# One-hot and gated columns of a routed expert layer, built on VectorE from 16-bit pairs

## The chip, the cores and the metric

The kernel runs on one core of a Trainium2 chip. The metric is device microseconds of one launch, as the median of repeated runs. One more run is taken with the hardware profiler, and all rows below come from it. The engines are named as the profile names them: PE (matmul) and PEld (its weight loads), DVE (VectorE), ACT (ScalarE), POOL (GpSimd) and SP (the queue that issues most loads).

## The reference

Two transformer-like blocks run over 256 tokens of width 1024. The change lies wholly in the last part, the routed feed-forward layer of the second block:

```python
def chunk(xc):
    q = (xc @ w_q).reshape(tc, PEER_HEADS, 2, PEER_DQ // 2)
    s = jnp.einsum('thpd,hpkd->thpk', q, sub_keys).astype(F32)
    s_top, i_top = lax.top_k(s, PEER_TOPK)
    ...
    best, pos = lax.top_k(cand.reshape(tc, PEER_HEADS, PEER_TOPK * PEER_TOPK), PEER_TOPK)
    expert = jnp.take_along_axis(...)
    gate = jax.nn.softmax(best, axis=-1)
    ue = jnp.take(expert_u, expert, axis=0)
    ve = jnp.take(expert_v, expert, axis=0)
    h = jax.nn.gelu(jnp.einsum('thkd,td->thk', ue, xc).astype(F32), approximate=False)
    return jnp.einsum('thk,thkd->td', (gate * h).astype(xc.dtype), ve)
```

Each token has 8 heads with 16 experts each, that is 128 slots. An expert's number is 128 i + j, with i and j from 0 to 127, and there are 16,384 experts.

## The kernel before

The kernel gathers nothing. It computes the gelu of all experts for all tokens, multiplies each by its gate (zero where the token has not chosen the expert), and multiplies the result with all of `peer_v`. H holds that table with i on the partitions and (j, token) behind it, in two halves of 64 values of j, H0 and H1.

The stages of `peer` are:

- **queries** and `up(0)`: the slots' i, j and gate are found on DVE (`top_experts`), while PE computes H0. At its end the slots stand on the partitions: `ir` and `jr` hold i and j of each slot by token, `gb` the gate in two 16-bit parts.
- **`up(1)`**: PE computes H1 with 24 matmuls of 256 columns for a weight unit pair (L312 to L315). Beside it `steps(0)` applies the gates to H0.
- **`down(0)`**: PE multiplies H0 with `peer_v` into four banks `acc` (L1390, 12 matmuls of 512 columns for a unit). Beside it `steps(1)` applies the gates to H1.
- **`down(1)`**: the same product for H1, with no gating left beside it, and then the last normalisation.

A step of gating serves 8 tokens. `spread` writes a one-hot column of i for each slot and token, A (128 by 8 by 128), and of j, B (128 by 8 by 64), both by comparing a row of the numbers 0 to 127 (`iota`, 32-bit, in the tile `keep`) with the slot's value; both comparisons are on DVE (L1429, L1431). POOL then makes B times the gate, once for each 16-bit part of the gate (G, L1435). `gated` multiplies A with the two G on PE, 16 small matmuls for 8 tokens (L1444), and DVE multiplies the result into H (L1446). There are 32 such steps for each half, and they come at 0.6 steps for each weight unit.

PE works in three 32-bit passes, so every operand is split into a high and a low part. For weights ACT makes the high part (`whi`, L205) and DVE the low one (`wlo`, L207), one of each for a unit of 128 by 1024, with three buffers of each. For H in `down`, ACT makes the high part (L1405) and POOL the low one (L1406), one of each for two units, in four places of the tiles `u3`. The first pair of H0 takes the two buffers of A for its parts, since `u3` still holds the input of `up(1)`.

In the queries stage the order of DVE and POOL is that of the code. In the experts stages (`up(1)`, `down`) a scheduler orders each engine's instructions; an engine then takes them strictly in that order.

Of the kernel before, what the change touches and what calls it, by code (L numbers as in the profile page):

```python
# [8 lines left out]
F32 = mybir.dt.float32  # L9
F32R = mybir.dt.float32r  # L10
BF16 = mybir.dt.bfloat16
F16 = mybir.dt.float16
U32 = mybir.dt.uint32
AF = mybir.ActivationFunctionType
OP = mybir.AluOpType
# [3 lines left out]
T = 256  # L19
# [5 lines left out]
UP = 2.0 ** 15  # L25
# [148 lines left out]
class Kern:  # L174
# [95 lines left out]
    def manual(self, scope, engines):  # L270

        names = dict(D=mybir.EngineType.DVE, A=mybir.EngineType.Activation, P=mybir.EngineType.Pool, T=mybir.EngineType.PE)
        if engines:
# [804 lines left out]
    def heads(self, m):  # L1078
# [33 lines left out]
        def level(lv):  # L1112
            A = act.tile([128, 4, C], F32, tag="Alv", name="Alv", bufs=5)
            nc.gpsimd.tensor_tensor(A, AT, b4(f"lvt{lv}"), op=OP.mult)
            return A

        nc.gpsimd.tensor_tensor(four(Wt), AT, b4("lvt0"), op=OP.mult)
        nc.gpsimd.tensor_tensor(four(Wt), b4("id64"), four(Wt), op=OP.subtract)
        A = level(1)
        nc.vector.transpose(out=W, in_=Wt)  # L1120
        yield HEADS[1]
        cut = lambda t, c, h: t[h, c * C:c * C + C]
        for lv in range(1, 6):
            p = self.two_banks(WARM_LEVEL)
            self.quads(lambda c, h, b, i: mm(p[h, b, i * C:i * C + C], A[h, c], cut(W, c, h), start=True, stop=True))
            X = act.tile([128, T], F32, tag="X", name="X", bufs=4)
# [69 lines left out]
    def chunks(self):  # L1196
# [6 lines left out]
        for c in range(4):  # L1203
# [15 lines left out]

            G = cut(self.sg, c)  # L1220
            if c:
                p = products((query(0), of(S0)))
                G = act.tile([128, 4, C], F32, tag="G", name="G", bufs=1)
                nc.vector.tensor_tensor(two(G), p, two(cut(self.sg, c)), op=OP.add)
                yield .5
# [130 lines left out]
    def peer(self, s):  # L1356
        tc, nc = self.tc, self.nc
# [3 lines left out]
        pp = e(tc.tile_pool(name="peer", bufs=1))  # L1361
# [5 lines left out]
        acc = [ps.tile([128, 512], F32, name=f"acc{i}") for i in range(4)]  # L1367


        ir, jr = (pp.tile([128, T], F16, name=n) for n in ("ir", "jr"))  # L1370
        gb = [pp.tile([128, T], F16, name=f"gb{n}") for n in range(2)]
        HJ = 64
        H = [None, None]
        H[0] = e(tc.tile_pool(name="h0", bufs=1)).tile([128, HJ, T], F32, name="H0")
        gp = e(tc.tile_pool(name="gp", bufs=1))
        mm = nc.tensor.matmul
# [15 lines left out]
        def down(half):  # L1392

            tail = []
            for i in range(HJ // 2):
                if half and i == HJ // 2 - 4:
                    nc.scalar.activation(ss[:, 0, 0:1], H[1][:, 2 * i, 0:1], AF.Square)
                    nc.scalar.activation(ss[:, 0, 0:1], ss[:, 0, 0:1], AF.Sqrt)
                if half == i == 0:
                    wh, wl = (gp.tile([128, 8, 128], F16, tag="A", name="A", bufs=2).rearrange("p a b -> p (a b)")  # L1400
                              .bitcast(F32R).rearrange("p (a t) -> p a t", a=2) for _ in range(2))
                else:
                    wh, wl = ((self.u3[n].rearrange("p (a b) t -> p a b t", b=2))[:, i % 4, :, :T] for n in range(2))
                src = H[half][:, 2 * i:2 * i + 2]
                nc.scalar.copy(wh, src)  # L1405
                nc.gpsimd.tensor_tensor(wl, src, wh.bitcast(F32), op=OP.subtract)  # L1406
                for u in range(2):
                    hi, lo = self.unit()
                    first = half + i + u == 0
                    todo = [(w[:, u], v) for w, v in ((wh, hi), (wl, hi), (wh, lo))]  # L1410
                    if half and i >= HJ // 2 - LAST:
                        tail.append(todo)
                        continue
                    for n, (w, v) in enumerate(todo):
                        for a in range(4):
                            products(a, w, v, first and n == 0, False)

            for a in range(4):
                for j, todo in enumerate(tail):
                    for n, (w, v) in enumerate(todo):  # L1420
                        products(a, w, v, False, j == len(tail) - 1 and n == 2)

        def spread(half, g):

            io, t8 = self.c("iota"), slice(g * 8, g * 8 + 8)
            A = gp.tile([128, 8, 128], F16, tag="A", name="A", bufs=2)
            B = gp.tile([128, 8, HJ], F16, tag="B", name="B", bufs=1)
            bc = lambda t, n: t[:, t8, None].to_broadcast([128, 8, n])
            nc.vector.tensor_tensor(B, io[:, None, half * HJ:half * HJ + HJ].to_broadcast([128, 8, HJ]),  # L1429
                                    bc(jr, HJ), op=OP.is_equal)  # L1430
            nc.vector.tensor_tensor(A, io[:, None, :].to_broadcast([128, 8, 128]), bc(ir, 128), op=OP.is_equal)  # L1431
            parts = []
            for n in range(2):
                G = gp.tile([128, 8, HJ], F16, tag=f"G{n}", name="G", bufs=2)
                nc.gpsimd.tensor_tensor(G, B, bc(gb[n], HJ), op=OP.mult)  # L1435
                parts.append(G)
            return A, parts

        def gated(half, g, A, parts):

            p = grp().rearrange("p (t j) -> p t j", t=8)
            for t in range(8):
                for n in range(2):
                    mm(p[:, t], A[:, t], parts[n][:, t], start=n == 0, stop=n == 1)  # L1444
            h = H[half][:, :, g * 8:g * 8 + 8]
            nc.vector.tensor_tensor(h, p.rearrange("p t j -> p j t"), h, op=OP.mult)  # L1446

# [46 lines left out]
        self.rest()  # L1494
        self.bg = steps(1)
        down(0)
        self.rest()
        self.save("H0", H[0])
# [42 lines left out]
    def top_experts(self, tk, sc, grp, ir, jr, gb, tt):  # L1541

        nc = self.nc
        v = nc.vector
# [21 lines left out]
        def pairs(h):  # L1566
            scr = tk.tile([128, 256], F32, tag="scr2", name="scr2", bufs=2)
            top16(bv[:, h], bi[:, h], cand[0][:, h], scr)
# [20 lines left out]
        def softmax():  # L1589
            g = tk.tile([128, 8, 16], F32, tag="gate", name="gate", bufs=1)  # L1590
            z = tk.tile([128, 8], F32, tag="z", name="z", bufs=1)
            v.tensor_tensor(g, bv, bv[:, :, 0:1].to_broadcast([128, 8, 16]), op=OP.subtract)
            nc.scalar.activation(g, g, AF.Exp)
            v.tensor_reduce(z, g, axis=AX.X, op=OP.add)
            v.reciprocal(z, z)
            v.tensor_tensor(g, g, z[:, :, None].to_broadcast([128, 8, 16]), op=OP.mult)

            def by_slot():
                p = grp()
                ts = slice(tt * 128, tt * 128 + 128)  # L1600
                nc.tensor.transpose(p[:, 0:128], g, self.c("ident"))
                nc.scalar.activation(gb[0][:, ts], p[:, 0:128], AF.Copy, scale=UP)
                v.scalar_tensor_tensor(gb[1][:, ts], p[:, 0:128], UP, gb[0][:, ts], op0=OP.mult, op1=OP.subtract)
            self.at(2, by_slot)
        yield COST[2], softmax

        def index(p2, dst):
            n = tk.tile([128, 8, 16], U32, tag="n", name="n", bufs=1)
            nf = tk.tile([128, 8, 16], F32, tag="nf", name="nf", bufs=2)
            out = tk.tile([128, 8, 16], F32, tag="nfo", name="nfo", bufs=2)  # L1610
            if p2 == 0:
                v.tensor_scalar(n, bi, 4, None, op0=OP.logical_shift_right)
            else:
                v.tensor_scalar(n, bi, 15, None, op0=OP.bitwise_and)
            v.tensor_copy(nf, n)

            def part(g):
                hs = slice(2 * g, 2 * g + 2)
                q = tk.tile([128, 2, 16, 16], F32, tag="pick", name="q", bufs=2)
                v.tensor_tensor(q.rearrange("p h k a -> p (h k) a"),  # L1620
                                nf[:, hs].rearrange("p h k -> p (h k)")[:, :, None].to_broadcast([128, 32, 16]),
                                io16[:, None, :].to_broadcast([128, 32, 16]), op=OP.is_equal)
                nc.gpsimd.tensor_tensor(q, q, tf[:, hs, p2][:, :, None, :].to_broadcast([128, 2, 16, 16]), op=OP.mult)
                return lambda: v.tensor_reduce(out[:, hs], q, axis=AX.X, op=OP.add)

            rest = []
            for g in range(5):
                yield
                if rest:
                    rest.pop()()  # L1630
                if g < 4:
                    rest.append(part(g))

            def by_slot():
                p = grp()
                nc.tensor.transpose(p[:, 0:128], out, self.c("ident"))
                nc.scalar.copy(dst[:, tt * 128:(tt + 1) * 128], p[:, 0:128])
            self.at(2, by_slot)

        for p2, dst in ((0, ir), (1, jr)):  # L1640
# [61 lines left out]
```

## Time and profile before

| what | value |
|---|---|
| median of 3 runs | 1479.79 us (1479.5 to 1481.15) |
| profiled execution, its own time | 1475.88 us |
| its span in the profile | 1474.1 us |
| PE busy | 1407.1 us (95%) |
| DVE busy | 1154.1 us (78%) |
| ACT busy | 721.2 us (49%) |
| POOL busy | 613.2 us (42%) |
| granted TensorE clock, mean | 0.980 |

The span runs from the first to the last instruction; 1.8 us of the run lie around it. The profiled execution is 3.9 us shorter than the median of the others, so a change worked out on its rows is to be taken off the median as a difference. Busy time of PE is modelled for pipelined matmuls: one that stands alone shows its whole latency as busy.

### The profile page before, as it was taken

The numbers are of one execution on the slowest core, as the hardware profiler recorded it, in microseconds if no ns is written. First come the engines' busy times: TensorE is split into PE (matmuls) and PEld (weight loads), VectorE is DVE, ScalarE is ACT, GpSimd is POOL, SyncE is SP. The second block draws the span as 40 slices with busy tenths as digits, with TensorE's granted clock in tenths as the row PEclk, the third lists the DMA queues.
The fourth block names the chain that finished last, engine by engine and source line by source line (L and its number), as shares of the span: only waits on it lengthen the run. The fifth ranks groups of instructions, "written<-read, shape, count | busy, mean of one in ns | idle before, by whom it ended". The sixth has DMA issues, their size and how long they took to land. (4 is left out here: it accounts for less than half of the span.)

```text
span 1474.1 us, 27562 instructions
## 1 busy us (share of the span) xinstructions
PE 1407.1 (95%) x11208; PEld 1284.0 (87%) x11208; DVE 1154.1 (78%) x1775; ACT 721.2 (49%) x1078; POOL 613.2 (42%) x434
## 2 busy tenths in 40 slices
PE   9999999999879999899999999999998898999997
PEld 7889999999768888899998999999976666788886
DVE  6789999974798766689879779999599999744445
ACT  6575566563763333645544543443543433445443
POOL 2601042210664200223465646777288887323230
PEclk9999999999989998999999999999999999999999
DMA  8478858744322101544544455444644455655552
GB/s 320 152 252 282 311 196 284 238 163 147 126 86 66 52 30 53 205 147 169 200 144 172 172 172 172 161 160 168 214 159 157 157 171 173 221 183 196 177 196 86
DMA packets 40447, 253.83 MB, mean 172 GB/s; under 512 B 4736, under 2 KB 4992, under 8 KB 13440
## 3 DMA queue, kind: packets, MB, share of 16 engines
q1 hardware_dynamic: 38592, 246.79, 48.4%
q10 hardware_dynamic: 1728, 5.28, 1.0%
q8 instruction: 88, 1.44, 0.4%
q14 instruction: 39, 0.32, 0.1%
HBM read 249.96 MB, written 2.10 MB: 171 GB/s over the span
## 5 line engine op out<-in xcount | busy, mean ns | idle before, releaser
L205 ACT CAST whi<-raw 128x1024 fp32r<-128x1024 f32 (+1 forms) x418 | 435.7, 1046 | 527.2 <-PE psu L313 217.9
L207 DVE TENSOR_TENSOR wlo<-raw,whi 128x1024 fp32r<-128x1024 f32 (+1 forms) x389 | 526.2, 1363 | 166.4 <-ACT whi L205 164.1
L312 PE MATMUL psu<-u3hi,whi 128*128 128x256 f32 x1128 | 287.2, 287 | 4.6 <-DVE qe L520 4.6
L313 PE MATMUL psu<-u3lo,whi 128*128 128x256 f32 x1128 | 282.9, 284 | 0.0
L1435 POOL TENSOR_TENSOR G<-B,gb 128x512 f16<-128x512 f16 x128 | 237.0, 1870 | 95.2 <-DVE B L1429 53.8
L312 PEld LDWEIGHTS psu<-u3hi,whi 128*128 128x128 f32 x1128 | 215.8, 191 | 4.8 <-DVE qe L520 4.8
L313 PEld LDWEIGHTS psu<-u3lo,whi 128*128 128x128 f32 x1128 | 215.6, 191 | 0.0
L315 PE MATMUL psu<-u3hi,wlo 128*128 128x256 f32 x1128 | 182.0, 284 | 4.1 <-DVE wlo L207 3.7
L1406 POOL TENSOR_TENSOR u3lo<-H,u3hi 128x512 fp32r<-128x512 f32 x63 | 106.8, 1696 | 160.0 <-ACT u3hi L1405 160.0
L315 PEld LDWEIGHTS psu<-u3hi,wlo 128*128 128x128 f32 x1128 | 155.5, 191 | 5.1 <-DVE wlo L207 4.2
L1390 PE MATMUL acc<-wlo,u3hi 128*128 128x512 f32 x504 | 141.7, 401 | 14.4 <-DVE wlo L207 14.0
L207 POOL TENSOR_TENSOR wlo<-raw,whi 128x1024 fp32r<-128x1024 f32 x29 | 70.5, 2430 | 188.2 <-ACT whi L205 188.2
L1390 PE MATMUL acc<-whi,u3hi 128*128 128x512 f32 x504 | 142.5, 402 | 1.9 <-ACT whi L205 1.9
L1390 PE MATMUL acc<-whi,u3lo 128*128 128x512 f32 x504 | 139.0, 396 | 0.0
L1390 PEld LDWEIGHTS acc<-wlo,u3hi 128*128 128x128 f32 x504 | 94.3, 190 | 42.7 <-DVE wlo L207 21.7
L1390 PEld LDWEIGHTS acc<-whi,u3lo 128*128 128x128 f32 x504 | 95.3, 189 | 22.1
L1390 PEld LDWEIGHTS acc<-whi,u3hi 128*128 128x128 f32 x504 | 93.3, 191 | 21.5 <-ACT whi L205 2.0
L1431 DVE TENSOR_TENSOR A<-keep,ir 128x1024 f16<-128x1024 f32 x64 | 94.9, 1484 | 0.1
L312 PE MATMUL mm<-u3hi,whi 128*128 128x256 f32 (+1 forms) x312 | 82.3, 295 | 0.0
L1429 DVE TENSOR_TENSOR B<-keep,jr 128x512 f16<-128x512 f32 x64 | 64.0, 1000 | 22.2 <-POOL G L1435 22.2
L313 PE MATMUL mm<-u3lo,whi 128*128 128x256 f32 (+1 forms) x312 | 78.7, 284 | 0.0
L313 PE MATMUL mm<-flo,whi 128*128 128x256 f32 x272 | 67.6, 282 | 0.0
(431 smaller groups left out, 2660.4 us busy)
## 6 DMA issues: line engine op xcount, KB each, us to landing
raw<-in_w_fm SPq DMA_DIRECT2D x74, 1024.0 KB, 4.9
raw<-in_peer_u SPq DMA_DIRECT2D x64, 1024.0 KB, 4.8
raw<-in_peer_v SPq DMA_DIRECT2D x64, 1024.0 KB, 4.8
ada<-in_ada_w SPq DMA_DIRECT2D x40, 512.0 KB, 5.4
raw<-in_w_qkv SPq DMA_DIRECT2D x5, 1024.0 KB, 10.6
H<-in_ada_w SPq DMA_DIRECT2D x8, 512.0 KB, 3.9
raw<-in_w_qkv SPq DMA_DIRECT2D x4, 256.0 KB, 5.2
xd<-kr SPq DMA_DIRECT2D x1, 1024.0 KB, 10.0
```

Source lines behind the costliest of these rows:

```text
L205: self.nc.scalar.copy(hi, src)
L207: e.tensor_tensor(lo, src, hi.bitcast(F32), op=OP.subtract)
L312: mm(out, w[k][0], x[k][0], start=start and k == 0, stop=False)
L313: mm(out, w[k][0], x[k][1], start=False, stop=False)
L315: mm(out, w[k][1], x[k][0], start=False, stop=stop and k == n - 1)
L1390: mm(acc[a], w[:, tt * 128:tt * 128 + 128], v[:, dh * 512:dh * 512 + 512], start=start, stop=stop)
L1406: nc.gpsimd.tensor_tensor(wl, src, wh.bitcast(F32), op=OP.subtract)
L1429: nc.vector.tensor_tensor(B, io[:, None, half * HJ:half * HJ + HJ].to_broadcast([128, 8, HJ]), bc(jr, HJ), op=OP.is_equal)
L1431: nc.vector.tensor_tensor(A, io[:, None, :].to_broadcast([128, 8, 128]), bc(ir, 128), op=OP.is_equal)
L1435: nc.gpsimd.tensor_tensor(G, B, bc(gb[n], HJ), op=OP.mult)
```

## The change

Three things change in `peer`:

- **All operands of A, B and G become 16-bit.** A 16-bit copy of `iota` is made once on ACT (the tile `io`). The slots' values `ir`, `jr` and `gb` are kept twice, side by side, so that a slot's value is read as a pair of equal neighbours again and again, in place of one element again and again. The writers of these values (L1602, L1603 and L1637 of before) write each value twice. `jr` and `gb` lie in the tile `qe`, which the queries stage has read by then. A, B and G are contiguous by token as before, written in pairs.
- **Both products G go from POOL to DVE**, right behind B or a step later.
- **The low part of H in `down`** (L1406) **goes from POOL to DVE** too.

```diff
-        ir, jr = (pp.tile([128, T], F16, name=n) for n in ("ir", "jr"))
-        gb = [pp.tile([128, T], F16, name=f"gb{n}") for n in range(2)]
+        ir = pp.tile([128, T, 2], F16, name="ir")
+        room = self.qe.rearrange("p a t -> p (a t)").bitcast(F16).rearrange("p (a t b) -> p a t b", a=3, b=2)
+        gb, jr = room[:, 0:2], room[:, 2]
+        io = pp.tile([128, 128], F16, name="io")
+        nc.scalar.copy(io, self.c("iota"))
...
-                nc.gpsimd.tensor_tensor(wl, src, wh.bitcast(F32), op=OP.subtract)
+                nc.vector.tensor_tensor(wl, src, wh.bitcast(F32), op=OP.subtract)
...
-            bc = lambda t, n: t[:, t8, None].to_broadcast([128, 8, n])
-            nc.vector.tensor_tensor(B, io[:, None, half * HJ:half * HJ + HJ].to_broadcast([128, 8, HJ]),
-                                    bc(jr, HJ), op=OP.is_equal)
-            nc.vector.tensor_tensor(A, io[:, None, :].to_broadcast([128, 8, 128]), bc(ir, 128), op=OP.is_equal)
-            parts = []
-            for n in range(2):
-                G = gp.tile([128, 8, HJ], F16, tag=f"G{n}", name="G", bufs=2)
-                nc.gpsimd.tensor_tensor(G, B, bc(gb[n], HJ), op=OP.mult)
-                parts.append(G)
-            return A, parts
+            G = gp.tile([128, 2, 8, HJ // 2, 2], F16, tag="G", name="G", bufs=2)
+            pairs = lambda t: t.rearrange("p (a b) -> p a b", b=2)[:, None]
+            of = lambda t, n: t[:, t8, None].to_broadcast([128, 8, n // 2, 2])
+            nc.vector.tensor_tensor(B, pairs(io[:, half * HJ:half * HJ + HJ]).to_broadcast([128, 8, HJ // 2, 2]),
+                                    of(jr, HJ), op=OP.is_equal)
             for n in range(2):
+                nc.vector.tensor_tensor(G[:, n], B, of(gb[:, n], HJ), op=OP.mult)
+            nc.vector.tensor_tensor(A, pairs(io).to_broadcast([128, 8, 64, 2]), of(ir, 128), op=OP.is_equal)
...
-                nc.scalar.activation(gb[0][:, ts], p[:, 0:128], AF.Copy, scale=UP)
-                v.scalar_tensor_tensor(gb[1][:, ts], p[:, 0:128], UP, gb[0][:, ts], op0=OP.mult, op1=OP.subtract)
+                two = p[:, 0:128, None].to_broadcast([128, 128, 2])
+                nc.scalar.activation(gb[:, 0, ts], two, AF.Copy, scale=UP)
+                v.scalar_tensor_tensor(gb[:, 1, ts], two, UP, gb[:, 0, ts], op0=OP.mult, op1=OP.subtract)
...
-                nc.scalar.copy(dst[:, tt * 128:(tt + 1) * 128], p[:, 0:128])
+                nc.scalar.copy(dst[:, tt * 128:(tt + 1) * 128], p[:, 0:128, None].to_broadcast([128, 128, 2]))
```

PE's order is the same in both kernels, but for two of the first matmuls of `down(0)`. What moves stands on DVE and POOL.

First, DVE in the middle of `down(0)`, one step of gating with the units around it. The order of before (`keep` holds the 32-bit `iota`; H_10167 is H1):

```order
L1446 TENSOR_TENSOR H_10167<-psg,H_10167 128x64x8
L1431 TENSOR_TENSOR A<-keep,ir 128x1024
L1429 TENSOR_TENSOR B<-keep,jr 128x512
L207 TENSOR_TENSOR wlo<-raw,whi 128x1024 x2
L1446 TENSOR_TENSOR H_10167<-psg,H_10167 128x64x8
```

The order after the change (`qe` is where `jr` and `gb` lie now; H_10166 is H1, H_7313 is H0):

```order
L1449 TENSOR_TENSOR H_10166<-psg,H_10166 128x64x8
L1438 TENSOR_TENSOR G<-B,qe 128x512 x2
L1439 TENSOR_TENSOR A<-io,ir 128x1024
L1435 TENSOR_TENSOR B<-io,qe 128x512
L207 TENSOR_TENSOR wlo<-raw,whi 128x1024
L1410 TENSOR_TENSOR u3lo<-H_7313,u3hi 128x2x256
L207 TENSOR_TENSOR wlo<-raw,whi 128x1024
L1449 TENSOR_TENSOR H_10166<-psg,H_10166 128x64x8
```

The two products and the low part of H now stand in DVE's queue, between the product into H and the low parts of the weights.

Second, POOL in `down(0)` before (gb_7309 and gb_7310 are the two parts of the gate, H_7314 is H0):

```order
L1435 TENSOR_TENSOR G<-B,gb_7309 128x512
L1435 TENSOR_TENSOR G<-B,gb_7310 128x512
L1406 TENSOR_TENSOR u3lo<-H_7314,u3hi 128x2x256
L1435 TENSOR_TENSOR G<-B,gb_7309 128x512
L1435 TENSOR_TENSOR G<-B,gb_7310 128x512
```

POOL's last instructions after the change, which all belong to the queries stage:

```order
L1627 TENSOR_TENSOR q<-q,tf 128x512
L207 TENSOR_TENSOR wlo<-raw,whi 128x1024
L1627 TENSOR_TENSOR q<-q,tf 128x512 x3
L207 TENSOR_TENSOR wlo<-raw,whi 128x1024 x2
L1693 UNCONDITIONAL_BRANCH
```

POOL has nothing left to do in `up(1)`, `down(0)` and `down(1)`.

Third, DVE around the start of `down(0)`. Before:

```order
L1446 TENSOR_TENSOR H_7314<-psg,H_7314 128x64x8
L1429 TENSOR_TENSOR B<-keep,jr 128x512
L207 TENSOR_TENSOR wlo<-raw,whi 128x1024 x12
L1431 TENSOR_TENSOR A<-keep,ir 128x1024 x2
L1446 TENSOR_TENSOR H_10167<-psg,H_10167 128x64x8
```

After:

```order
L1449 TENSOR_TENSOR H_7313<-psg,H_7313 128x64x8
L1438 TENSOR_TENSOR G<-B,qe 128x512 x2
L1410 TENSOR_TENSOR A<-H_7313,A 128x512
L1435 TENSOR_TENSOR B<-io,qe 128x512
L207 TENSOR_TENSOR wlo<-raw,whi 128x1024 x10
L1410 TENSOR_TENSOR u3lo<-H_7313,u3hi 128x2x256 x2
L207 TENSOR_TENSOR wlo<-raw,whi 128x1024
L1410 TENSOR_TENSOR u3lo<-H_7313,u3hi 128x2x256 x2
L207 TENSOR_TENSOR wlo<-raw,whi 128x1024
L1439 TENSOR_TENSOR A<-io,ir 128x1024 x2
L1449 TENSOR_TENSOR H_10166<-psg,H_10166 128x64x8
```

The first low parts of H, which can be made only when `up(1)` has left `u3`, stand ahead of two low parts of weights now; on POOL nothing stood behind them but products of the gates.

## Rows read from the trace of the kernel before

**Rows 1.** Page, busy tenths in 40 slices of 36.9 us: PE, DVE, POOL.

```profile
PE   9999999999879999899999999999998898999997
...
DVE  6789999974798766689879779999599999744445
...
POOL 2601042210664200223465646777288887323230
```

**Rows 2.** Windows: start:end, length, busy us (count) of PE, PEld, DVE, ACT, POOL; clock.

```profile
861.00:1057.90 196.90, 196.90 (x2023) 195.41 (x2022) 172.28 (x157) 82.75 (x97) 120.21 (x66) 1.00 0.49 168
1057.90:1258.40 200.50, 178.66 (x1168) 135.77 (x1168) 186.97 (x152) 77.42 (x90) 164.81 (x90) 0.98 0.48 166
1258.40:1285.00 26.60, 26.60 (x109) 21.49 (x110) 20.98 (x22) 11.51 (x13) 6.14 (x5) 0.94 0.66 233
1285.00:1462.50 177.50, 177.50 (x772) 143.99 (x771) 77.22 (x64) 82.69 (x94) 48.98 (x29) 1.00 0.51 175
```

**Rows 3.** Waits, 1057 to 1260: waiter, releaser, total us, times, longest us.

```profile
PEld acc L1390 <- DVE wlo L207: 21.7, 18, 3.1
...
PE acc L1390 <- DVE wlo L207: 14.0, 13, 2.6
...
PEld L1444 <- DVE A L1431: 9.2, 12, 1.4
```

**Rows 4.** Chain of waits, 1057 to 1474: start us, us, what.

```profile
1065.55 0.64 PE psg L1444 x16
...
1071.37 0.48 PE psg L1444 x16
...
1258.37 76.72 PE acc L1390 x324
...
1335.97 126.49 PE acc L1390 x546
```

**Rows 5.** Groups by form, DVE, 1057.9 to 1258.4: busy us, mean ns, idle before.

```profile
L207 DVE TENSOR_TENSOR wlo<-raw,whi 128x1024 fp32r<-128x1024 f32 x53 | 83.0, 1584 | 2.6 <-ACT whi L205 2.6
L1431 DVE TENSOR_TENSOR A<-keep,ir 128x1024 f16<-128x1024 f32 x32 | 48.8, 1527 | 0.1
L1429 DVE TENSOR_TENSOR B<-keep,jr 128x512 f16<-128x512 f32 x29 | 37.9, 1307 | 10.3 <-POOL G L1435 10.3
L1446 DVE TENSOR_TENSOR H<-psg,H 128x512 f32<-128x512 f32 x30 | 20.3, 678 | 0.0
L496 DVE SCALAR_TENSOR_TENSOR H<-H 128x1024 f32<-128x1024 f32 x4 | 7.5, 1868 | 0.7 <-DMA H<-in_ada_w 0.7
```

**Rows 6.** Groups by form, POOL, the same stretch.

```profile
L1435 POOL TENSOR_TENSOR G<-B,gb 128x512 f16<-128x512 f16 x60 | 114.2, 1922 | 32.8 <-DVE B L1429 19.9 <-PE psg L1444 10.4 <-PE acc L1390 2.5
L1406 POOL TENSOR_TENSOR u3lo<-H,u3hi 128x512 fp32r<-128x512 f32 x30 | 52.0, 1736 | 26.7 <-ACT u3hi L1405 26.7
```

**Rows 7.** Timeline, DVE, 967 to 978: start us, us, instruction.

```profile
967.54 0.68 DVE L1446 TENSOR_TENSOR H<-psg,H 128x512 f32<-128x512 f32 x1
968.15 1.46 DVE L1431 TENSOR_TENSOR A<-keep,ir 128x1024 f16<-128x1024 f32 x1
969.52 0.68 DVE L1429 TENSOR_TENSOR B<-keep,jr 128x512 f16<-128x512 f32 x1
...
975.22 0.68 DVE L1429 TENSOR_TENSOR B<-keep,jr 128x512 f16<-128x512 f32 x1
975.82 1.21 DVE L207 TENSOR_TENSOR wlo<-raw,whi 128x1024 fp32r<-128x1024 f32 x1
976.96 0.68 DVE L1446 TENSOR_TENSOR H<-psg,H 128x512 f32<-128x512 f32 x1
```

**Rows 8.** Line L1429, 1057 to 1260: count, duration min/median/max ns.

```profile
L1429 DVE TENSOR_TENSOR B<-keep,jr x29: 676/1656/1684, 1070.5 to 1248.8; 128x512 f16<-128x512 f32 x29
```

**Rows 9.** Line L1435, the same stretch and columns.

```profile
L1435 POOL TENSOR_TENSOR G<-B,gb x60: 1039/2014/2023, 1066.2 to 1252.4; 128x512 f16<-128x512 f16 x60
```

**Rows 10.** Line L207, 130 to 160: an instruction of a quarter of wlo's size.

```profile
L207 DVE TENSOR_TENSOR mlo<-t,mhi x8: 410/412/418, 135.0 to 154.1; 128x256 fp32r<-128x256 f32 x8
```

More of the change, by code (lines that the diff above doesn't have):

```diff
@@ L1399, in down @@
                 if half == i == 0:
-                    wh, wl = (gp.tile([128, 8, 128], F16, tag="A", name="A", bufs=2).rearrange("p a b -> p (a b)")
+                    wh, wl = (gp.tile([128, 8, 64, 2], F16, tag="A", name="A", bufs=2).rearrange("p a b c -> p (a b c)")
                               .bitcast(F32R).rearrange("p (a t) -> p a t", a=2) for _ in range(2))
@@ L1423, in spread, with gated @@
         def spread(half, g):
-            io, t8 = self.c("iota"), slice(g * 8, g * 8 + 8)
-            A = gp.tile([128, 8, 128], F16, tag="A", name="A", bufs=2)
-            B = gp.tile([128, 8, HJ], F16, tag="B", name="B", bufs=1)
-            bc = lambda t, n: t[:, t8, None].to_broadcast([128, 8, n])
-            nc.vector.tensor_tensor(B, io[:, None, half * HJ:half * HJ + HJ].to_broadcast([128, 8, HJ]),
-                                    bc(jr, HJ), op=OP.is_equal)
-            nc.vector.tensor_tensor(A, io[:, None, :].to_broadcast([128, 8, 128]), bc(ir, 128), op=OP.is_equal)
-            parts = []
-            for n in range(2):
-                G = gp.tile([128, 8, HJ], F16, tag=f"G{n}", name="G", bufs=2)
-                nc.gpsimd.tensor_tensor(G, B, bc(gb[n], HJ), op=OP.mult)
-                parts.append(G)
-            return A, parts
-        def gated(half, g, A, parts):
+            t8 = slice(g * 8, g * 8 + 8)
+            A = gp.tile([128, 8, 64, 2], F16, tag="A", name="A", bufs=2)
+            B = gp.tile([128, 8, HJ // 2, 2], F16, tag="B", name="B", bufs=1)
+            G = gp.tile([128, 2, 8, HJ // 2, 2], F16, tag="G", name="G", bufs=2)
[3 more added lines that the diff above has]
+                                    of(jr, HJ), op=OP.is_equal)
+            for n in range(2):
+                nc.vector.tensor_tensor(G[:, n], B, of(gb[:, n], HJ), op=OP.mult)
+            nc.vector.tensor_tensor(A, pairs(io).to_broadcast([128, 8, 64, 2]), of(ir, 128), op=OP.is_equal)
+            return A.rearrange("p t a b -> p t (a b)"), G.rearrange("p n t a b -> p n t (a b)")
+        def gated(half, g, A, G):
             p = grp().rearrange("p (t j) -> p t j", t=8)
@@ L1443, in gated @@
                 for n in range(2):
-                    mm(p[:, t], A[:, t], parts[n][:, t], start=n == 0, stop=n == 1)
+                    mm(p[:, t], A[:, t], G[:, n, t], start=n == 0, stop=n == 1)
             h = H[half][:, :, g * 8:g * 8 + 8]
```

## The prediction

> **What bounds the kernel now.** I read the busy slices first: PE is full nearly everywhere, and among its few dips those between slices 29 and 34 fall where DVE and POOL are both heavily loaded [rows 1]. I then cut the experts stages into windows [rows 2]. In `up(1)` (861 to 1057.9) PE is busy for all of 196.9 us: PE is the bound, although DVE works 172 us and POOL 120 us beside it. In `down(0)` (the window to 1258.4, when the last gating product is done) PE is busy for 178.66 of 200.5 us, DVE for 186.97 and POOL for 164.81. In `down(1)` PE is full again. So the only stretch in which this change can give much is `down(0)`. The waits there say who holds PE: mostly DVE's low parts of weights, 14.0 us seen by the matmuls and 21.7 us by their weight loads, and then A [rows 3]. PE waits for DVE, not for data from memory.
>
> How much is there? PE's pace when nothing holds it is 126.49 us for 546 `acc` matmuls, 0.2317 us each; 870 of the 1536 of both halves come after 1258.37, so 666 stand in the stretch [rows 4]: 154.3 us. The 32 groups of 16 gating matmuls take 0.48 to 0.64 us [rows 4]; with 0.56, between them, 17.9 us. PE needs 172.2 us and gets 200.5. The room is 28.3 us, more than the 21.8 us of idle time that the window shows, since a burst behind each stall shows its latency as busy.
>
> Why is DVE late, with no instruction in it that takes that long? B lasts 0.68 us at the least and 1.66 in the median of this stretch [rows 8]; G on POOL 1.04 at the least and 2.01 in the median [rows 9]; a low part of weights 1.21 us when free [rows 7] and 1.58 in the mean here [rows 5]. The surplus of one is about the length of the other's instruction: they hold each other up. H, whose one operand is in PSUM, keeps its 678 ns [rows 5].
>
> **The change, part by part.** Costs are start to start, since an instruction overlaps the end of the one before [rows 7]: B 0.60 to 0.61 (969.52 to the next, 975.22 to 975.82), `wlo` 1.14 (975.82 to 976.96), H 0.61, and A behind H 1.37 (968.15 to 969.52), which is 0.23 more than `wlo` of the same size; I charge that 0.23 to whatever follows H.
>
> *Removed:* POOL's 60 G and 30 low parts of H in the stretch, 166 us busy [rows 6], and with them everything that made DVE's own instructions long. I take POOL's share as wholly gone, since nothing of it is left in these stages.
>
> *DVE's new load in the stretch.* What stays: 53 `wlo` at 1.14 = 60.4; 32 H at 0.61 = 19.5, and 32 times 0.23 = 7.4; 4 of L496 at their present 1.87 = 7.5, which is generous. What is added: 30 low parts of H, two SBUF operands of 128x512 like B's, at 0.61 = 18.3. Together 113.1 us.
>
> Then the 16-bit work: 32 steps with one B and two G (96 instructions of 512 elements) and one A of 1024. No row shows DVE with two 16-bit SBUF operands and a 16-bit result, so I bound it. Above: no gain from 16 bits, as B of today with one 32-bit operand, 0.61; A as `wlo`, 1.14: 58.6 + 36.5 = 95.1 us. Below: half the elements' time, which is that of the 32-bit instruction with the same bytes: 128x256 lasts 0.41 [rows 10], less the same overlap of 0.07 gives 0.34; A as 128x512, 0.61: 32.6 + 19.5 = 52.1 us. I take the lower one, because the edit removes just what sets B apart from it, the 32-bit operand and the single repeated element, and leaves every operand in neighbouring pairs; that is a choice, not a row. [...]
>
> So DVE has 165.2 us of work (lower bound) or 208.2 (upper) against PE's 172.2.
>
> At the lower bound PE is the bound again, with DVE 96% loaded. I leave 5 us for what doesn't fit: L496 is bunched in the last 20 units, and DVE's queue is strict. The stretch becomes 177 instead of 200.5: 23.5 us. Behind it PE's clock was down to 0.94 for 26.6 us [rows 2], and 324 matmuls took 0.2368 us instead of 0.2317 [rows 4], 1.6 us; PE without stalls ahead should keep its clock, so I add 1.5. Sum: **25 us**.
>
> *At nothing:* the 16-bit copy of `iota`, the doubled values (six small writes on ACT, two on DVE) and the first two steps' G, in the queries stage, behind matmuls. `up(1)`: DVE's load there falls, but PE was full, so no gain; at the lower bound it costs nothing either.
>
> *New waits.* The low parts of H stand in DVE's one queue now. At the start of `down(0)` two of them wait for `up(1)`'s last matmul and ACT's cast, with one low part of weights behind, for the third unit. That is done some 3.3 us after `up(1)`'s end (a cast at the mean of ACT's instructions there, 77.42 us over 90 [rows 2], 0.9; two at 0.61; `wlo` 1.21), and PE comes to it after two units of 12 matmuls, 5.6 us: hidden by 2 us. Without that cover it would cost up to 3.3 us, once. H waits for PE's gating matmuls, as before, with G, A, B behind it instead of A and B: 0.7 us more in front of the next `wlo`, which has three buffers, so two units, ahead.
>
> **Rivals.**
> *DVE stays the bound in part.* The pair of a slot's value is the same four bytes read again up to 64 times; should the engine step more slowly over such an operand, or the strict queue cost half the stalls, DVE ends near the middle of the bounds, 186.7 us in the stretch: 13.8 us off, time 1466. Against: today's B re-reads one element 64 times, and at 0.68 it is as fast as H, which re-reads nothing [rows 7]. For: DVE has 4% of air. [...]
>
> *Slower: the pairs bring nothing.* At the upper bound DVE needs 208.2 us in `down(0)`, 7.7 more than now. In `up(1)`, the 55 units with gating have 55 times 2.83 us of PE (196.9 less 16 for the gating, over 64 units) plus 16, 171.5 us; DVE has 55 times 1.14, and 19.5 + 7.4 + 95.1: 184.7, or 13 more. Together 21 us more: 1501. Between the bounds it decides at three quarters of the way, about 0.55 us start to start for 512 elements (0.61 lasting). For it speaks that B's 16-bit result and slot values save nothing today.
>
> *No change:* the same crossing, or PE held by something that DVE's lateness now hides. ACT (77 of 200) is far from it [rows 2].
>
> **How the numbers follow.** Forecast 0.72; DVE in part 0.14; slower 0.08; within 0.2% 0.03; a larger gain, up to the whole 28.3 + 1.6 = 30 us (1450) and a few us from the queries stage, 0.03. Less than 0.2% (3 us) can hardly be told from no change. The profiled run of 1475.9 would become 1450.9; the median of 1479.8 lies 3.9 above it, and less 25 is **1455**. The range runs from 1447 (all the room, and 3 us besides) to 1470, beyond the partial case; it leaves out the slow end. Faster 0.88, same 0.04, slower 0.08.
>
> **What the profile after would show.** B and G at about 0.41 us and A at 0.68 on DVE (else 0.68 and 1.21, and the slower rival); `wlo` at 1.21 throughout `down(0)`, with POOL empty; `down(0)`'s gating over some 177 us after its start, with PE's waits for `wlo` down to a few us; the matmuls behind it at 0.232 us. `up(1)` should stay at 197 us. The prediction fails if PE still waits there for something else, most likely `wlo` behind H or L496.

## The result and the profile after

The changed kernel takes 1441.52 us in the median of 4 runs (1439.72 to 1444.46); the kernel before, run beside it, 1479.64 us (1475.83 to 1481.15). The ratio is 0.9747, with a 95% interval of 0.9730 to 0.9764: 38 us faster, by the interval 35 to 40. The forecast was 25 us faster, 1455 us, with a range from 1447; the time lies under that range.

The busy slices of the changed kernel, to be held against [rows 1]:

```profile
PE   9999999999869999989998999999999999999997
...
DVE  5779999994598875769978867878679999655555
...
POOL 1800032220285210022456440000000000000000
```

POOL is empty from slice 24 on (counted from 0), and the dips of PE in slices 29 to 34 are gone. The windows by stage (busy time and count of PE, PEld, DVE, ACT, POOL, then the granted clock, as in [rows 2], then what the DMA engines did). The first is the end of the queries stage, from the first gate to up(1)'s first gating product; then up(1), down(0) to its last gating product, and the 26.6 us behind it:

```profile
738.30:862.80 124.50, 118.68 (x987) 116.98 (x986) 95.23 (x146) 58.69 (x73) 67.58 (x37) 1.00 0.51 177
862.80:1060.10 197.30, 197.30 (x2026) 195.86 (x2025) 147.55 (x224) 83.11 (x98) 0.00 (x0) 1.00 0.49 167
1060.10:1228.30 168.20, 168.20 (x1162) 133.80 (x1161) 152.94 (x243) 75.89 (x89) 0.00 (x0) 1.00 0.60 204
1228.30:1254.90 26.60, 26.60 (x122) 21.58 (x119) 19.93 (x25) 11.93 (x14) 0.00 (x0) 1.00 0.65 217
```

The gated stretch of down(0) fell from 200 to 168 us, and PE is busy for all of it, at a granted clock of 1.00. DVE has 153 us of work there, 91%. The groups by form on DVE in that stretch (busy us, mean ns), as in [rows 5]:

```profile
L207 DVE TENSOR_TENSOR wlo<-raw,whi 128x1024 fp32r<-128x1024 f32 x55 | 67.3, 1223 | 13.4 <-ACT whi L205 13.0 <-issue 0.2
L1438 DVE TENSOR_TENSOR G<-B,qe 128x512 f16<-128x512 f16 x60 | 22.5, 417 | 0.0
L1439 DVE TENSOR_TENSOR A<-io,ir 128x1024 f16<-128x1024 f16 x32 | 21.9, 684 | 0.6 <-PE acc L1394 0.6
L1449 DVE TENSOR_TENSOR H<-psg,H 128x512 f32<-128x512 f32 x31 | 21.2, 683 | 1.3 <-PE psg L1447 1.3
L1410 DVE TENSOR_TENSOR u3lo<-H,u3hi 128x512 fp32r<-128x512 f32 x28 | 18.7, 685 | 0.0
L1435 DVE TENSOR_TENSOR B<-io,qe 128x512 f16<-128x512 f16 x29 | 12.1, 418 | 0.0
```

G and B last 0.417 us, as the 32-bit instruction of half the elements does [rows 10], and A 0.684 us. A low part of weights is back at 1.22 us from 1.58. Of PE's instructions, only the weight loads of the gating products appear among the waits of the stretch (7.1 us of issue time, 1.1 us for DVE's low parts of H); no matmul waits for anything.

### The profile page after: what moved, and what is told of

It is laid out like the page before. It is cut to its first block, busy times and chain, and to the rows that moved or that the text cites. A ratio compares the mean times of both kernels' runs of the same rounds, so it can differ in the third digit from the quotient of the medians.

```text
span 1442.7 us, 27290 instructions
## 1 busy us (share of the span) xinstructions
PE 1400.3 (97%) x11208; PEld 1284.6 (89%) x11208; DVE 1110.6 (77%) x1967; ACT 719.0 (50%) x1079; POOL 269.6 (19%) x242
## 5 line engine op out<-in xcount | busy, mean ns | idle before, releaser
L207 DVE TENSOR_TENSOR wlo<-raw,whi 128x1024 fp32r<-128x1024 f32 (+1 forms) x389 | 488.3, 1259 | 197.1 <-ACT whi L205 196.1
L312 PE MATMUL psu<-u3hi,whi 128*128 128x256 f32 x1128 | 285.6, 286 | 4.4 <-DVE qe L520 4.4
L313 PE MATMUL psu<-u3lo,whi 128*128 128x256 f32 x1128 | 281.3, 283 | 0.0
L312 PEld LDWEIGHTS psu<-u3hi,whi 128*128 128x128 f32 x1128 | 214.5, 190 | 4.6 <-DVE qe L520 4.6
L313 PEld LDWEIGHTS psu<-u3lo,whi 128*128 128x128 f32 x1128 | 214.2, 190 | 0.0
L1394 PE MATMUL acc<-wlo,u3hi 128*128 128x512 f32 x504 | 138.2, 394 | 0.0
L207 POOL TENSOR_TENSOR wlo<-raw,whi 128x1024 fp32r<-128x1024 f32 x29 | 72.0, 2483 | 190.5 <-ACT whi L205 190.5
L312 PE MATMUL mm<-u3hi,whi 128*128 128x256 f32 (+1 forms) x312 | 82.3, 295 | 0.0
L313 PE MATMUL mm<-u3lo,whi 128*128 128x256 f32 (+1 forms) x312 | 78.7, 284 | 0.0
L313 PE MATMUL mm<-flo,whi 128*128 128x256 f32 x272 | 67.6, 282 | 0.0
L312 PE MATMUL mm<-fhi,whi 128*128 128x256 f32 x272 | 67.6, 282 | 0.0
L312 PEld LDWEIGHTS mm<-u3hi,whi 128*128 128x128 f32 x312 | 59.5, 191 | 3.2 <-issue 2.5
L312 PE MATMUL mm<-n3hi,whi 128*128 128x256 f32 (+1 forms) x160 | 48.3, 326 | 14.0 <-DVE kr L960 9.4
L313 PEld LDWEIGHTS mm<-u3lo,whi 128*128 128x128 f32 x312 | 59.5, 191 | 0.3 <-issue 0.2
```

The costliest lines, as they stand in the source:

```text
L207: e.tensor_tensor(lo, src, hi.bitcast(F32), op=OP.subtract)
L312: mm(out, w[k][0], x[k][0], start=start and k == 0, stop=False)
L313: mm(out, w[k][0], x[k][1], start=False, stop=False)
L1394: mm(acc[a], w[:, tt * 128:tt * 128 + 128], v[:, dh * 512:dh * 512 + 512], start=start, stop=stop)
```

## The experiments

All times below are in us. Each kernel ran beside the kernel before, and the ratio is to that. The stage times are read from the profiles by three marks: the first gate's write, the first and the last gating product, and the first `acc` matmul. "Start" is what lies ahead of the scores in the queries stage, which no kernel here touches. Between it and the first gate lie 106.1 to 106.2 us in every profile, which the table leaves out.

| run | start | gate to up(1) | up(1) | down(0), gated | rest | median | ratio (95%) |
|---|---|---|---|---|---|---|---|
| before, first profile | 627.2 | 127.9 | 197.3 | 199.9 | 215.7 | 1479.64 | |
| e1 before again | 632.1 | 129.3 | 197.4 | 201.3 | 214.1 | 1480.65 | 1.0006 (0.9990 to 1.0021) |
| after, first profile | 632.1 | 124.5 | 197.3 | 168.4 | 214.2 | 1441.52 | 0.9747 (0.9730 to 0.9764) |
| e2 after again | 627.7 | 124.5 | 197.4 | 168.3 | 214.2 | 1444.27 | 0.9770 (0.9749 to 0.9791) |
| e3 single element | 627.6 | 128.3 | 199.6 | 194.1 | 214.1 | 1473.97 | 0.9965 (0.9948 to 0.9981) |
| e4 H's low part on POOL | 632.1 | 124.5 | 197.4 | 169.3 | 214.1 | 1443.16 | 0.9741 (0.9701 to 0.9781) |
| e5 G on POOL | 627.7 | 127.2 | 197.3 | 170.8 | 215.4 | 1447.36 | 0.9792 (0.9763 to 0.9821) |
| e6 pairs alone | 625.3 | 127.2 | 197.3 | 177.7 | 214.1 | 1454.47 | 0.9841 (0.9808 to 0.9873) |
| e7 H's low part alone on DVE | 632.4 | 127.9 | 197.4 | 195.8 | 214.1 | 1474.76 | 0.9962 (0.9946 to 0.9979) |
| e8 selection in pairs too | 633.1 | 117.7 | 197.3 | 168.4 | 214.2 | 1437.16 | 0.9709 (0.9677 to 0.9742) |
| e9 after, five rounds | 632.8 | 124.5 | 197.3 | 168.4 | 214.2 | 1444.44 | 0.9754 (0.9730 to 0.9779) |
| e10 e8, five rounds | 632.8 | 117.7 | 197.3 | 168.4 | 214.2 | 1435.88 | 0.9703 (0.9679 to 0.9728) |

The start varies between 625 and 633 us in kernels that do not differ there, so two profiles can differ by several microseconds without cause; the other stages repeat within 0.2 us for one kernel where PE doesn't wait, and within 1.6 us where it does.

**e1, e2 and e9: how much of a difference is chance.** The two kernels, unchanged.

> The kernel before, unchanged, to see how much of the difference between two profiles is chance. Theory A (the gain beyond the gated stretch was a clock dip that comes and goes): the stretch from the first gate (about 735 us) to the first gating product of up(1) again takes anything from 122 to 127 us, with a granted clock that differs from the first profile's 0.97. Theory B (the four early products on POOL hold that stretch up): again 126 us at 0.97 or lower. Both: down(0)'s gated stretch again 198 to 202 us, time 1476 to 1481.

> The changed kernel, unchanged, beside it. Both theories: 1439 to 1445 us, gated stretch of down(0) 168 to 169.5 us. Theory A: the stretch from the first gate to up(1)'s first gating product varies between 122 and 127 us here too; theory B: 122 to 123.5.

> The changed kernel once more beside the next one on one chip. If the stage times of the profiles are all there is (127.9 to 129.3 us before up(1) down to 124.5, 199.9 to 201.3 us in down(0) down to 168.3): 35 to 38 us under the kernel before, ratio 0.974 to 0.977.

The changed kernel's stage ahead of up(1) took 124.5 us in all three of its profiles, at a clock of 1.00, and that of before 127.9 and 129.3, at 0.97 and 0.96. (The expectations count this stage from a mark 1.7 us later.) So the 3.4 to 4.8 us there belong to the change, and theory A falls. The record of the granted clock has two levels in these traces, 1.0 and 0.5, and a share between them is a window with some of both. At 0.5 matmuls of 256 columns start 0.21 us apart (L312 and L313, 788.63 to 790.13 in the first profile of before), at 1.0 0.12 us (790.95 to 791.78). The kernel before in windows of 10 us, two of them, shows where the difference lies:

```profile
763.30:773.30 10.00, 8.08 (x56) 7.82 (x56) 7.37 (x9) 2.87 (x4) 7.77 (x5) 0.84 0.32 107
...
783.30:793.30 10.00, 6.34 (x42) 6.13 (x41) 9.50 (x22) 1.92 (x3) 5.70 (x5) 0.83 0.21 67
```

The same two places in the changed kernel, 5 us later in its run:

```profile
768.30:778.30 10.00, 8.38 (x69) 7.97 (x68) 7.35 (x7) 4.01 (x5) 7.85 (x5) 1.00 0.33 113
...
788.30:798.30 10.00, 7.67 (x64) 7.46 (x64) 9.72 (x26) 3.16 (x4) 3.48 (x4) 1.00 0.40 117
```

PE stalls at both places in both kernels, but the clock fell only before the change, with 56 and 42 matmuls done in 10 us against 69 and 64. PE's idle time in the whole stage differs by only 0.7 us (6.55 of 127.9 against 5.82 of 124.5); the rest is matmuls at the lower clock. By the trace's record of the clock, it stood at 0.5 for 6.8 us of this stage in the first profile of before and for 10.2 us in e1, and never in the changed kernel's three; half of that, 3.4 and 5.1 us as an estimate, is about what the stage lost.

**e3: one element in place of the pair.** All operands stay 16-bit; a slot's value is read with step 0 innermost.

```diff
-            of = lambda t, n: t[:, t8, None].to_broadcast([128, 8, n // 2, 2])
+            of = lambda t, n: t[:, t8, 0:1].to_broadcast([128, 8, n])
...
```

> The change, but a slot's value is read as one 16-bit element again and again (step 0 innermost) in place of a pair; all operands are 16-bit still. Theory 1 (the pair is what halves the time): B and G 0.68 us, A 1.21; DVE then needs about 153.5 + 32*(3*0.26 + 0.53) = 195 us in the stretch of down(0) and the time is 1475 to 1490. Theory 2 (16-bit operands do it, however they are walked): B and G 0.42, A 0.68, time 1440 to 1445.

The groups on DVE in its down(0):

```profile
L207 DVE TENSOR_TENSOR wlo<-raw,whi 128x1024 fp32r<-128x1024 f32 x54 | 66.1, 1226 | 7.4 <-PE acc L1394 4.5 <-ACT whi L205 2.7
L1440 DVE TENSOR_TENSOR A<-io,ir 128x1024 f16<-128x1024 f16 x32 | 39.1, 1224 | 0.4 <-PE acc L1394 0.4
L1439 DVE TENSOR_TENSOR G<-B,qe 128x512 f16<-128x512 f16 x60 | 38.8, 691 | 0.0
```

G lasts 0.691 and A 1.224 us, where the kernels with the 32-bit operand have 0.68 for 512 elements (B in e7) and 1.21 for A (e7 with POOL idle): sixteen bits alone save nothing here, the pair does. Theory 1 holds for the durations; the time, 1474 us, lies just under its 1475 to 1490. DVE is the bound of that stretch: 186.3 us busy of 194.1, and PE waits for G, all but 0.9 us of it in down(0):

```profile
PE psg L1448 <- DVE G L1439: 13.6, 10, 2.7
```

Yet the kernel is 0.35% faster than before (0.19 to 0.52 by the interval), not slower: this is the slower rival put to the test, and it comes out on the other side.

**e4 to e7: the parts by themselves.** e4 gives H's low part back to POOL (the first edit below), e5 the products G (the second), e6 both, and e7 is the kernel before with H's low part on DVE (the first edit the other way round).

```diff
-                nc.vector.tensor_tensor(wl, src, wh.bitcast(F32), op=OP.subtract)
+                nc.gpsimd.tensor_tensor(wl, src, wh.bitcast(F32), op=OP.subtract)
...
-                nc.vector.tensor_tensor(G[:, n], B, of(gb[:, n], HJ), op=OP.mult)
+                nc.gpsimd.tensor_tensor(G[:, n], B, of(gb[:, n], HJ), op=OP.mult)
```

> The change, but the low part of H stays on POOL. If moving it gave part of the gain (POOL and DVE hold each other up): DVE's low parts of weights grow again to a mean of 1.5 us in down(0), and the time is 1446 or more. If the gated stretch has room for it: DVE is less loaded by 18 us and lengthened by at most 30 times about 0.9 us = 27 us, in all below PE's 168.5 us, and the time is 1439 to 1445.

> The change, but both products G stay on POOL (16-bit pairs; A, B and H's low parts on DVE as changed). Theory 1 (instructions with two SBUF operands on DVE and POOL exclude each other, so their times add): DVE 54 wlo at 1.14, 32 A at 0.61, 29 B at 0.34, 28 low parts at 0.61, and POOL 60 G at 1.04, in all 170.5 us against PE's 168.3: down(0) 172 to 185 us, time 1446 to 1460, with G at 1.8 us or more in the mean. Theory 2 (only DVE's load counts, and it falls by 20 us): down(0) 168 to 169.5 us, time 1439 to 1446. In the queries stage, from the first gate to up(1)'s first gating product: 127 us or more if the four early G on POOL hold it up, 124.5 if not.

> The 16-bit pairs alone: G and H's low parts both stay on POOL, A and B are made as changed. Theory 1 (times of DVE and POOL add): 61.6 + 19.5 + 10 on DVE, 62.4 + 30*1.18 = 97.8 on POOL, 189 us: down(0) 185 to 195 us, time 1459 to 1472. Theory 2 (DVE's own load decides): 168 to 170 us, 1440 to 1446.

> The kernel before with only H's low parts on DVE. Theory 1 (times add): 61.6 + 36.5 + 17.7 + 18.3 on DVE and 62.4 on POOL, 196 us, against 214 by the same sum before, which took 200 to 201: down(0) 184 to 197 us, time 1464 to 1477. Theory 2 (DVE's load decides): DVE's own work, alone 154 us with H, rises by 18 us on an engine that was 94% busy: slower, 1484 or more.

From before to e6, the pairs alone take 22 to 24 us out of down(0) (199.9 and 201.3 to 177.7). Moving H's low part on top, e6 to e5, takes 6.9; moving G instead, e6 to e4, 8.4; both, 9.3. Once G is on DVE, where H's low part runs hardly matters: e4 and the changed kernel differ by 0.9 us in the stretch and not beyond the intervals in time. In the kernel before, that move alone is worth 4 to 5.5 us (e7).

Theory 2 of these runs falls by e7: DVE took on 18 us of work, was busier than before by no more than 0.7 us (187.41 of 195.6 against 186.77 of 199.7), and the kernel got faster. What counted is the work that both engines do on two SBUF operands: in the kernel before, by the trace, an instruction of that kind was in flight on one engine or the other for 199 of the 199.9 us of down(0)'s gated stretch. But theory 1, that these times simply add, is right only in part. It gave 196 us for e7 (195.8 came) and 170.5 for e5 (170.8 came, though I had written 172 to 185 for it, for waits, and 1.8 us for G, which took 1.65 in the mean), but 189 for e6, where 177.7 came, and the same sum gives 214 for the kernel before, which took 199.9 and 201.3. The hit in e7 is luck: for 12 us of its stretch no such instruction was in flight. That in e5 says little, since PE alone needs 168.2 us. DVE's groups in e6, most of down(0):

```profile
L207 DVE TENSOR_TENSOR wlo<-raw,whi 128x1024 fp32r<-128x1024 f32 x57 | 87.3, 1554 | 1.6 <-ACT whi L205 1.6
L1435 DVE TENSOR_TENSOR B<-io,qe 128x512 f16<-128x512 f16 x29 | 32.9, 1133 | 9.4 <-POOL G L1438 9.4
L1439 DVE TENSOR_TENSOR A<-io,ir 128x1024 f16<-128x1024 f16 x32 | 31.0, 970 | 0.1
```

B, which lasts 0.418 us with POOL idle, takes 1.133 in the mean here and 1.402 in the median: a B that meets a G on POOL loses nearly all of that G (1.04 us at the least). What runs side by side is little; the last section has its size. The queries stage sorts as well: with G on POOL and the rest in pairs (e5, e6) it takes 127.2 us, with all on DVE at full duration (e3) 128.3, with all on DVE in pairs 124.5 (e2, e4, e9). So the pairs alone give 0.7 to 2.1 us there, and G's move 2.7 more. The stall of PE that DVE's `wlo` ends lasts 4.3 us in e5 and 2.3 in the changed kernel, and the clock stood at 0.5 for 3.4 us in e5 and e6, for 6.8 in e3.

**e8 and e10: a version that beats both.** The wait left at the end of the queries stage is an exchange between DVE and POOL of the same kind: DVE compares (L1624), POOL multiplies (L1627), DVE reduces. Here the same pairs are used for it, all on DVE:

```diff
-            nf = tk.tile([128, 8, 16], F32, tag="nf", name="nf", bufs=2)
+            nf = tk.tile([128, 8, 16, 2], F16, tag="nf", name="nf", bufs=2)
...
-                q = tk.tile([128, 2, 16, 16], F32, tag="pick", name="q", bufs=2)
+                q = tk.tile([128, 2, 16, 16], F16, tag="pick", name="q", bufs=2)
...
+                                nf[:, hs].rearrange("p h k b -> p (h k) b")[:, :, None].to_broadcast([128, 32, 8, 2]),
+                                io16[:, None].to_broadcast([128, 32, 8, 2]), op=OP.is_equal)
...
-                nc.gpsimd.tensor_tensor(q, q, tf[:, hs, p2][:, :, None, :].to_broadcast([128, 2, 16, 16]), op=OP.mult)
+                v.tensor_tensor(q, q, tf[:, hs, p2][:, :, None, :].to_broadcast([128, 2, 16, 16]), op=OP.mult)
```

> Beyond the change: the selection of the slots' i and j at the end of the queries stage (comparison with 0 to 15 and product with the found indices) in 16-bit pairs on DVE too, the product off POOL. If PE's last stalls there (5.8 us, waits for wlo and for the reductions behind POOL's product) come from that exchange between DVE and POOL: the stretch from the first gate to up(1) falls from 124.5 to 119 to 122 us, time 1437 to 1441 or 3 to 5 us under the changed kernel. If DVE's load in that stretch is the cause: no difference beyond 1.5 us.

> The change with the selection of i and j in 16-bit pairs on DVE too. If the 6.8 us that its profile showed before up(1) (117.7 against 124.5) are real: 5 to 8 us under the changed kernel, ratio to the kernel before 0.969 to 0.972. If they were chance: the same as the changed kernel within 2 us.

The window from the first gate to up(1) in e8:

```profile
739.30:857.00 117.70, 116.94 (x986) 116.69 (x984) 93.57 (x162) 58.40 (x73) 39.80 (x21) 1.00 0.55 187
```

The wait of PE that is left in it (total us, count, longest):

```profile
PE psu L315 <- DVE wlo L207: 0.8, 1, 0.8
```

PE is idle for 0.8 us where it was for 5.8. The stage shrinks by 6.8 us, more than the 2.5 to 5.5 expected, and DVE's busy time hardly moves (95.23 to 93.57): it was not DVE's load. POOL's fell from 67.58 to 39.80 us, so whether DVE's waiting for POOL's product or the two engines' holding each other up weighed more is not shown. On one chip, e10 took 1435.88 and e9 1444.44 us, 8.6 us less where 5 to 8 were expected, and the two intervals of the ratio do not meet.

## Why the prediction was wrong in size

The place, the mechanism and the sign were right; the sum of 25 us was too small, by three of its terms. In profiles without the start, the change gives 3.4 + 31.5 + 1.5 = 36.4 us against the first profile of before, and 4.8 + 32.9 - 0.1 = 37.6 against e1.

- **What bounds it** held: down(0) was the only stage of the experts stretch that changed, PE bounds it now, and up(1) stayed at 197.3 us, as said.
- **The room in down(0)**, 28.3 us: mis-sized by 4. PE needs 168.2 us there, not 172.2. The pace and the price of a gating group were right: 648 matmuls at 0.2317 are 150.1 us, and the 18.1 left are 0.565 us a group, where 0.56 was put. (In the chain after the change a group takes 0.48 us, and the `acc` matmuls behind it 0.08 to 0.10 more than their pace, 5.64 us for 24.) The count was wrong. It was 1536 less the 870 matmuls that the chain shows after 1258.37; but the chain leaves PE for the last normalisation on DVE at 1462.48, and 18 `acc` matmuls still come behind that. So 648 and not 666 stand in the stretch, which is 4.2 us. The window of the kernel before with `acc` alone has them (649, one of them cut by the window's edge), and the chain after shows the groups. Not all of what down(0) gave was idle time: by the trace's record the clock stood at 0.5 for 6.8 us there in the first profile of before and for 10.2 in e1, which costs about half of that as an estimate, and never after the change.

```profile
1057.90:1258.40 200.50, 164.93 (x649) 119.70 (x650) 0.98 0.48 166
...
1066.36 5.64 PE acc L1394 x24
1072.00 0.48 PE psg L1447 x16
```

- **The reserve of 5 us** "for what doesn't fit" was the largest single miss: nothing was left. I had DVE at 96%, and it was 91%, since two prices were too high. The 0.23 us behind each H, 7.4 us in all, are not H's: in the changed kernel the instruction behind H starts 0.60 us after it and two G take 0.67 us together, as priced without it. They were POOL's, whose share the prediction had itself taken as wholly gone: in [rows 7] a G on POOL still runs for 0.37 us beside the A behind H (the last section has the rows). L496 lasts 1.22 us with POOL idle, not the 1.87 that I called generous. These are the timeline rows of the changed kernel:

```profile
1129.67 0.68 DVE L1449 TENSOR_TENSOR H<-psg,H 128x512 f32<-128x512 f32 x1
1130.27 0.75 DVE L1438 TENSOR_TENSOR G<-B,qe 128x512 f16<-128x512 f16 x2
1130.94 0.68 DVE L1439 TENSOR_TENSOR A<-io,ir 128x1024 f16<-128x1024 f16 x1
1131.54 0.42 DVE L1435 TENSOR_TENSOR B<-io,qe 128x512 f16<-128x512 f16 x1
1131.88 1.22 DVE L207 TENSOR_TENSOR wlo<-raw,whi 128x1024 fp32r<-128x1024 f32 x1
```

- **The 16-bit prices** were right at the lower bound: B 0.34, G 0.33 and A 0.60 us start to start here (0.34, 0.34 and 0.61 forecast).
- **"At nothing ... in the queries stage"** is the step that failed as a statement: the first two steps' columns weigh 3.4 to 4.8 us there, 2.7 of it by G's move off POOL (e5) and the rest by the pairs (e6). I priced G as work on DVE and not as what it does on POOL to DVE's `wlo`, to PE's stalls and to the clock, which fell in this stage with stalls of 1.9 and 3.7 us before and with none of the changed kernel's. The stall that DVE's `wlo` ends was 3.7 us before, and 4.3 with G alone back on POOL (e5); after the change the longest is 2.3.
- **The clock behind down(0)**, 1.5 us: right against the first profile, whose clock fell to 0.94 there; in e1 it did not fall, so there was nothing to win. That part comes and goes.
- **The new waits** stayed hidden: no wait of PE at the start of down(0).
- **The rivals.** DVE as the bound in part did not happen: the pair read again cost next to nothing, 0.417 us for 512 elements against 0.412 of the 32-bit row of the same bytes [rows 10]. The slower rival was over-priced: at full duration (e3) the kernel takes 1474, not 1501, since down(0) took 194.1 us and not 208.2, and up(1) lost 2.3 us and not 13.

## What to carry to other kernels

Where two engines lengthen each other's instructions, as DVE and POOL did here (B 0.418 us with POOL idle, 1.133 in the mean of e6), price a move between them by the minimum of each duration, and read the bound by the engine that waits for both: here PE, busy for all of down(0)'s 168.2 us. Nothing of the stalls then remained, so a reserve needs a row of its own. Count instructions in a window and not along the chain of waits, which can leave an engine before its work ends. A 16-bit operand that is the same for many elements should be stored as a pair and walked as pairs; it cut 512 elements from 0.69 to 0.42 us here, and 16 bits without it saved nothing (0.69 against 0.68). A stage with short stalls of PE was worth more than its idle time here, since the clock fell with them: 3.4 us, of which 0.7 were idle.

## What the hardware showed that I had not expected

- DVE and POOL with two SBUF operands each held each other up in these traces, almost wholly; H, with one operand in PSUM, kept its 0.68 us beside them (0.676 to 0.685 before, 61 of its 64 with POOL at work). As an estimate, such work at its least, start to start (G 1.00 and H's low part 1.14 us on POOL), adds up to 208 us in down(0) before, 189 in e7 and 182 in e6 (L496 left out); one engine or the other had it in flight for 199, 184 and 174 us. So adding up as if nothing ran side by side comes out 3 to 5% too high.
- A compared column A of 1024 elements behind H took 1.46 us before the change and 1.22 in e3. POOL makes the difference, and not the 32-bit operand or H: in e7, where A is as before and POOL has gaps, all 42 that start behind H beside a running G last 1.454 to 1.460 us, and all 15 with POOL idle 1.205 to 1.209. The A of [rows 7] starts at 968.15, when the second G of this POOL row has 0.37 us left:

```profile
964.65 3.87 POOL L1435 TENSOR_TENSOR G<-B,gb 128x512 f16<-128x512 f16 x2 [0.87 <-DVE B L1429]
```

A loses 0.25 of these 0.37 us, so only some 0.12 us run side by side. Two rows of e7, the first with POOL idle:

```profile
1105.00 1.21 DVE L1431 TENSOR_TENSOR A<-keep,ir 128x1024 f16<-128x1024 f32 x1
...
1108.47 1.46 DVE L1431 TENSOR_TENSOR A<-keep,ir 128x1024 f16<-128x1024 f32 x1
```

- In the stage ahead of up(1), PE stood idle for 1.9 and 3.7 us in the two windows of before in which the granted clock was 0.84 and 0.83; with 1.6 and 2.3 us at the same places, the changed kernel kept 1.00.
